# Gates as Strassen block products of normed inputs, kept in DRAM, with the state-space chunks between them

## The chip, the cores and the metric

One Trainium2 chip, one NeuronCore of it. A kernel's time is device microseconds of one execution; "before" is the median of three runs, and one further execution was profiled.

## The reference

One decoder layer on x of 1024 tokens by 1024 columns, float32. Cut to what matters here:

```python
h = rms_norm(x, norm1_g)
proj = h @ w_in                       # columns: u | q (3 groups) | k | v | conv input | g (3 x 1024)
y_s = s5_branch(u, ...)               # diagonal complex state space, gelu, @ w_ssm_glu, GLU
y_a = dilated_attention(q, k, v) @ w_att_up
y_c = conformer_conv(cv, ...)         # GLU, 31-tap causal conv, LayerNorm, silu, @ w_conv_pw2
gate = sigmoid(g + b_gate).reshape(bsz, seq, 3, 1024)
merged = gate[:, :, 0] * y_s + gate[:, :, 1] * y_a + gate[:, :, 2] * y_c
x = x + merged @ w_out
h = rms_norm(x, norm2_g)
z = h @ w_ffn_in
x = x + (silu(z[..., :2816]) * z[..., 2816:]) @ w_ffn_out
out = rms_norm(x, final_g)
```

## The kernel before

Tokens lie along the free axis (two halves of 512), features along the 128 partitions; a 1024-column operand is eight tiles of 128x1024. Every product is computed to float32 accuracy from float32r parts: each operand is split into a high part (ScalarE copy, `whi`) and the rest (subtraction on GpSimd or VectorE, `wlo`), and three matmuls, high by high, high by low and low by high, are summed in PSUM (`gemms`, L191 to L205). One block of weights is four 128x128 tiles: one load, one ScalarE copy (L104), one GpSimd subtraction (L105), and then 24 matmuls of 512 columns when both halves of the tokens are done.

The stages, in the order of the program: the input norm (`norm1`, L317), whose right sides are `hh` and `hl`, x times its gain and not yet divided by the root mean square; that factor, `rb`, is multiplied in when a product leaves PSUM. Then, for four pairs of heads, projections, attention (`attend0`, `attend1`), the 31-tap convolution on VectorE (`conv`, 31 operations of 1024 columns for each quarter) and the merge of the attention groups (`merge`, L499). Then the input of the state space (`project_u`, L609), the tables of its rotations (`s5_tables`, L778), the convolution's LayerNorm (`conv_norm`, L573, traced at high priority), and the stage of the state space (`s5_stage`, L632). This last one runs eight chunks of the state space (`s5`, L800, a generator with four parts: coefficients; transposes and kernel; states and scans; outputs) in between units of branch work, the number of units in a chunk given by `SHARE`. A unit is one 128-column block of a branch with its gate: `gate` (L920) is 48 matmuls on `hh`, `hl`, a VectorE multiplication by `rb` and a ScalarE tanh for each half, and the branch's own product is 24 matmuls. Branch c (convolution) and a (attention) are done so; branch s (state space, 48 matmuls for the two halves of its GLU) follows alone (`branch_s`, L960). There are 24 gates, eight for each branch. Then the output projection, the second norm, and the feed-forward part.

The feed-forward part already uses Strassen's scheme in Winograd's form on pairs of blocks: `left_sides` (L114) makes four sums of weight blocks for each pair (VectorE, L127) and splits seven left operands, `wino` (L152) runs seven block products of 12 matmuls into four PSUM banks, `right_sides` and `norm2` (L1015) make the sums of the token halves. Plainly done, the same pair takes 96 matmuls; so done, 84.

The order on each engine is made by a planner from the program's order as priority and an estimate of each operation's time; each engine then works its list strictly in order. `issue_after` ties instructions behind a given one on its engine. Loads and stores are issued in order by SP's queue, a few by ScalarE's. Tiles come from pools stacked from the left and from the right of the memory; a tile that takes the place of an older one waits until that one has been read for the last time.

Of the kernel before, what the change touches and what calls it, by code (L numbers as in the profile page):

```python
# [28 lines left out]
GAHEAD = 4  # L29
SHARE = (2, 2, 4, 2, 1, 2, 1, 1)  # L30
# [56 lines left out]
class Body:  # L87
    def __init__(self, tc, ins, out):
        self.tc, self.nc, self.i, self.out = tc, tc.nc, ins, out
        nc = tc.nc  # L90
        self.V, self.A, self.G, self.PE = nc.vector, nc.scalar, nc.gpsimd, nc.tensor
        self.ahead = []
        self.bufs = {"wraw": 2, "whi": 3, "wlo": 3, "t2": 4, "g": 4, "s": 2, "pt": 1, "pv": 1, "l": 16}
# [151 lines left out]
    def run(self):  # L245
        tc, nc, V, A, G, PE = self.tc, self.nc, self.V, self.A, self.G, self.PE
        with ExitStack() as st:
# [3 lines left out]
            early, banks = ExitStack(), ExitStack()  # L251
            self.wp = early.enter_context(tc.tile_pool(name="w", bufs=1, side="right", reuse_waits="tile"))
            self.pp = banks.enter_context(tc.tile_pool(name="ps", bufs=1, space=PSUM, reuse_waits="tile"))
            self.consts()
            pool = lambda name, side="left": tc.tile_pool(name=name, bufs=1, side=side, reuse_waits="tile")
            right = ExitStack()
            with pool("s5c") as self.sc, pool("h") as self.hp:
# [3 lines left out]
                with pool("at4") as self.ap4, pool("at1") as self.ap1, pool("at2") as self.ap2, pool("at3") as self.ap3, pool("at5") as self.ap5:  # L261
# [6 lines left out]
                    for hp in range(HP):  # L268
# [13 lines left out]
                self.mp = right.enter_context(pool("mg", "right"))  # L282
                with pool("gt") as self.gp, pool("br") as self.bp:
                    self.mg = [self.mp.tile([P, T], F32, tag="mg", name=f"mg{m}", bufs=KD + 1) for m in range(KD)]
# [7 lines left out]
                    self.lp = right.enter_context(pool("ml", "right"))  # L292
                    self.branch_s()
            self.lp2 = enter(pool("left"))
            self.out_proj()
            right.close()
            banks.close()
            self.bufs = {"wraw": 6, "wsum": 3, "whi": 4, "wlo": 4, "t2": 8, "ct": 6, "g": 6, "s": 2, "l": 16, "r": 20}
            self.wp = enter(pool("w2"))
            self.pp = enter(tc.tile_pool(name="ps2", bufs=1, space=PSUM, reuse_waits="tile"))  # L300
            self.early, self.enter = early, enter
            self.ffn()
            self.fill(self.rp2, 32)
# [13 lines left out]
    def norm1(self):  # L317
        nc, V, A, G, PE = self.nc, self.V, self.A, self.G, self.PE
        with self.tc.tile_pool(name="xin", bufs=1, reuse_waits="tile") as xp:
# [14 lines left out]
            self.hh = [self.hp.tile([P, T], F32R, name=f"hh{k}") for k in range(KD)]  # L334
            self.hl = [self.hp.tile([P, T], F32R, name=f"hl{k}") for k in range(KD)]
# [208 lines left out]
    def conv_in(self, ct):  # L544
        A, V = self.A, self.V
        if ct == 0:
            self.cx = {}
# [3 lines left out]
        cx = self.cx[ct] = self.ap3.tile([P, TAPS - 1 + T], F32, tag="cx", name="cx", bufs=2)  # L551
        self.G.memset(cx[:, 0:TAPS - 1], 0.0)
# [9 lines left out]
    def conv(self, ct):  # L562
        V = self.V
        cx = self.cx[ct]
# [8 lines left out]
    def conv_norm(self):  # L573
        A, V, G, PE = self.A, self.V, self.G, self.PE
        self.acts = self.act_tiles()
        for h in range(2):
            t = slice(512 * h, 512 * h + 512)
# [3 lines left out]
            ss = self.vp.tile([P, 512], F32, tag="css", name="css", bufs=2)  # L581
            V.tensor_tensor(out=ss, in0=cy[0], in1=cy[1], op=ALU.add)
            for ct in (2, 3):
                V.tensor_tensor(out=ss, in0=ss, in1=cy[ct], op=ALU.add)
            mu = self.psum("s")
            PE.matmul(mu, self.ones, ss, start=True, stop=True)
            ss = self.vp.tile([P, 512], F32, tag="css", name="css", bufs=2)
# [8 lines left out]
            bc = self.rstd([ss], BW)  # L596
# [688 lines left out]
```

## Time and profile before

| | |
|---|---|
| median of three runs | 1868.55 us (1859.29 to 1868.56) |
| the profiled execution | 1869.71 us, its span 1867.9 us |
| mean granted TensorE clock | 0.971 |
| TensorE matmuls | 8524, busy 96% of the span |
| VectorE, ScalarE, GpSimd busy | 64%, 36%, 42% |
| HBM read, written | 149.57 MB, 55.54 MB |

Spans inside the trace are counted from its first instruction. TensorE's matmuls overlap in the record: a row's duration is longer than the distance from one start to the next. A clock of 1.00 is 2.4 GHz, and 0.50 is 1.2 GHz. The stages: input norm and first projections up to about 130 us, attention to about 550, `project_u` to about 600, gates with state-space chunks to about 905, branch s to about 1080, output projection to about 1190, feed-forward to the end.

### The profile page before, as it was taken

How to read it: one execution, taken by the hardware profiler on the slowest of the kernel's cores; microseconds unless marked ns; L12 is line 12 of the kernel's file. 1: busy time of each engine (PE TensorE's matmuls, PEld its weight loads, DVE VectorE, ACT ScalarE, POOL GpSimd, SP SyncE). 2: the span in 40 equal slices, each digit the busy share in tenths (PEclk: the TensorE clock that was granted, in tenths of full speed). 3: DMA queues.
4: the chain of work that ended last, by engine and by line, in shares of the span. 5: the costliest groups of instructions: out<-in, count | busy, mean ns of one | idle time of the engine just before them, and what ended most of it. 6: DMA issues, size and time to landing. Idle time of an engine off the chain costs nothing. (4 is left out here: it accounts for less than half of the span.)

```text
span 1867.9 us, 24041 instructions
## 1 busy us (share of the span) xinstructions
PE 1798.2 (96%) x8524; PEld 1415.7 (76%) x8524; DVE 1203.5 (64%) x2010; ACT 673.1 (36%) x1280; POOL 775.7 (42%) x649
## 2 busy tenths in 40 slices
PE   7989999999999999999999999989999999999997
PEld 5867675766757778888888888757888888788876
DVE  7964767837757674764343332798888777755556
ACT  5303314223240432322332333544454555533332
POOL 5522222322222153444322234764555555467671
PEclk9989899989999899999999999989999999999998
DMA  4430110210104232322311154313444444477752
GB/s 165 131 101 30 40 57 12 68 51 11 52 18 151 69 92 78 96 81 75 95 57 51 45 186 141 130 51 119 153 158 147 163 153 164 162 269 270 266 177 90
DMA packets 118248, 206.69 MB, mean 111 GB/s; under 512 B 12264, under 2 KB 53864, under 8 KB 118128
## 3 DMA queue, kind: packets, MB, share of 16 engines
q1 hardware_dynamic: 114224, 198.86, 31.6%
q10 hardware_dynamic: 3904, 6.29, 0.9%
q8 instruction: 67, 1.10, 0.2%
q14 instruction: 53, 0.43, 0.1%
HBM read 149.57 MB, written 55.54 MB: 110 GB/s over the span
## 5 line engine op out<-in xcount | busy, mean ns | idle before, releaser
L105 POOL TENSOR_TENSOR wlo<-wraw,whi 128x512 fp32r<-128x512 f32 x185 | 256.4, 1387 | 575.8 <-ACT whi L104 565.5
L202 PE MATMUL ps<-hh,whi 128*128 128x512 f32 x832 | 338.3, 407 | 9.1 <-ACT whi L104 6.5
L204 PE MATMUL ps<-hh,wlo 128*128 128x512 f32 x832 | 334.8, 403 | 8.5 <-POOL wlo L105 8.5
L203 PE MATMUL ps<-hl,whi 128*128 128x512 f32 x832 | 337.3, 406 | 4.1 <-DVE hl L340 4.1
L104 ACT ACTIVATE whi<-wraw 128x512 fp32r<-128x512 f32 x183 | 115.4, 631 | 503.2 <-PE ps L203 391.3
L166 PE MATMUL ps<-f,whi 128*128 128x512 f32 x616 | 242.5, 394 | 5.4 <-DVE f L111 3.2
L165 PE MATMUL ps<-f,whi 128*128 128x512 f32 x616 | 242.0, 393 | 5.1 <-ACT f L110 3.3
L111 POOL TENSOR_TENSOR wlo<-wsum,whi 128x512 fp32r<-128x512 f32 (+2 forms) x144 | 187.3, 1303 | 126.4 <-ACT whi L110 66.1
L202 PEld LDWEIGHTS ps<-hh,whi 128*128 128x128 f32 x832 | 161.4, 194 | 49.1 <-issue 9.2
L204 PEld LDWEIGHTS ps<-hh,wlo 128*128 128x128 f32 x832 | 161.0, 193 | 48.2 <-POOL wlo L105 8.9
L203 PEld LDWEIGHTS ps<-hl,whi 128*128 128x128 f32 x832 | 161.2, 194 | 42.1 <-DVE hl L340 6.1
L111 POOL TENSOR_TENSOR wlo<-wraw,whi 128x512 fp32r<-128x512 f32 (+2 forms) x107 | 140.8, 1317 | 122.6 <-ACT whi L110 67.0
L569 DVE SCALAR_TENSOR_TENSOR cy<-cx,hcw,cy 128x1024 f32<-128x1024 f32 x120 | 167.8, 1398 | 0.7
L168 PE MATMUL ps<-f,wlo 128*128 128x512 f32 x616 | 166.4, 392 | 0.0
L166 PEld LDWEIGHTS ps<-f,whi 128*128 128x128 f32 x616 | 116.5, 189 | 32.9 <-DVE f L111 4.7
L165 PEld LDWEIGHTS ps<-f,whi 128*128 128x128 f32 x616 | 116.4, 189 | 32.4 <-ACT f L110 5.4
L168 PEld LDWEIGHTS ps<-f,wlo 128*128 128x128 f32 x616 | 116.8, 190 | 24.2
L110 ACT ACTIVATE whi<-wsum 128x512 fp32r<-128x512 f32 (+2 forms) x144 | 83.1, 579 | 100.5 <-PE ps L166 83.7
L165 PE MATMUL ps<-g,whi 128*128 128x512 f32 x280 | 110.0, 393 | 3.5 <-DMA g<-ad 3.1
L166 PE MATMUL ps<-g,whi 128*128 128x512 f32 x280 | 109.6, 392 | 0.0
L111 DVE TENSOR_TENSOR g<-ct,g 128x512 fp32r<-128x512 f32 x79 | 78.6, 1002 | 44.0 <-ACT g L110 43.9
L202 PE MATMUL ps<-ah,whi 128*128 128x512 f32 x256 | 99.8, 390 | 0.0
(280 smaller groups left out, 3197.9 us busy)
## 6 DMA issues: line engine op xcount, KB each, us to landing
ad<-g SPq DMA_DIRECT2D x65, 512.0 KB
g<-ad SPq DMA_DIRECT2D x65, 512.0 KB
wraw<-in_win SPq DMA_DIRECT2D x120, 256.0 KB
wraw<-in_wffi SPq DMA_DIRECT2D x96, 256.0 KB
wraw<-in_wffo SPq DMA_DIRECT2D x48, 192.0 KB
wraw<-in_wout SPq DMA_DIRECT2D x32, 256.0 KB
wraw<-in_wglu SPq DMA_DIRECT2D x16, 256.0 KB
xa<-in_xt SPq DMA_DIRECT2D x8, 512.0 KB
```

The costliest lines, as they stand in the source:

```text
L104: eng.tensor_copy(hi, raw) if eng else self.A.activation(hi, raw, AF.Copy)
L105: self.G.tensor_tensor(out=lo, in0=raw, in1=hi.bitcast(F32), op=ALU.subtract)
L110: self.A.activation(hi, src, AF.Copy)
L111: eng.tensor_tensor(out=lo, in0=src, in1=hi.bitcast(F32), op=ALU.subtract)
L165: PE.matmul(o, hi[:, k, :], xh, start=first and k == 0, stop=False, skip_group_check=not first)
L166: PE.matmul(o, hi[:, k, :], xl, start=False, stop=False, skip_group_check=not first)
L168: self.mm = PE.matmul(o, lo[:, k, :], xh, start=False, stop=k == n - 1, skip_group_check=not first).ins
L202: self.PE.matmul(o, hi[:, k, :], xh[k0 + k][:, t], start=first, stop=False)
L203: self.PE.matmul(o, hi[:, k, :], xl[k0 + k][:, t], start=False, stop=False)
L204: self.mm = self.PE.matmul(o, lo[:, k, :], xh[k0 + k][:, t], start=False, stop=last).ins
L569: V.scalar_tensor_tensor(out=cy, in0=cx[:, j:j + T], scalar=self.hcw[:, ct * TAPS + j:ct * TAPS + j + 1], in1=cy, op0=ALU.mult, op1=ALU.add)
```

## The change

The gates are computed in twelve pairs of 128-column blocks, each as seven block products on sums of the normed inputs: four row blocks of x are read from DRAM again, multiplied by gain and `rb`, summed, and split (`early_sides` for products 5, 6 and 4 during `project_u`; `late_sides` for 1, 2, 3 and 7 after it, in the place of `hh` and `hl`). Gates go through a tanh to DRAM (`gd`, stored from ScalarE's queue) and are loaded again in the branches, which now come after all gates, in the order a, s, c. The chunks of the state space run between the block products of gates, eight products to a chunk. The tables of rotations are made before the last merge; the convolution's norm is made in steps between the units of branches a and s. The weights' pool of the feed-forward part (six raw buffers, four `whi`, four `wlo`) is opened before `project_u`, so the old one of two, three and three ends there. The convolution's two padded inputs become fixed tiles, zeroed once.

```diff
+GATES = tuple((8 * b + m, 8 * b + m + 1) for b in (1, 0, 2) for m in range(0, 8, 2))
+CHUNK = 8
...
+                        else:
+                            self.s5_tables()
                         if hp % 2:
                             self.merge(hp // 2)
                         self.conv(hp)
+                early.close()
+                self.bufs.update({"wraw": 6, "wsum": 3, "whi": 4, "wlo": 4, "t2": 8, "ct": 6, "l": 16, "r": 20})
+                self.wp = enter(pool("w2", "right"))
+                self.tp = right.enter_context(pool("t", "right"))
+                with pool("xn") as self.xp, pool("uw") as self.up:
                     self.project_u()
-                    with pool("tb") as self.sp:
-                        self.s5_tables()
-                    with pool("cn") as self.vp:
-                        with tc.high_priority():
-                            self.conv_norm()
-                    with pool("s5") as self.sp:
-                        self.s5_stage()
-                    self.branch_s()
+                    begun = self.first_products()
+                    for p in (1, 2, 3):
+                        self.late_sides(p)
+                with pool("s5") as self.sp:
+                    self.gate_stage(begun)
+                self.bp = right.enter_context(pool("br", "right"))
+                self.acts_a()
+                self.last_gates()
+            self.mp = left.enter_context(pool("mg"))
+            with pool("cn") as self.vp:
+                self.branches()
+            self.lp = left.enter_context(pool("ml"))
+            self.last_branch()
...
+    def block(self, k, h):
+        b = self.xp.tile([P, 512], F32, tag="xb", name="xb", bufs=8)
+        self.nc.sync.dma_start(out=b, in_=self.i["xt"][k][:, HALVES[h]])
+        return b, k, h
+    def normed(self, block):
+        b, k, h = block
+        self.V.scalar_tensor_tensor(out=b, in0=b, scalar=self.vec(C_N1 + k), in1=self.rb[:, HALVES[h]], op0=ALU.mult, op1=ALU.mult)
+        return b
+    def early_sides(self, blocks):
+        V = self.V
+        b11, b12, b21, b22 = (self.normed(b) for b in blocks)
+        V.tensor_tensor(out=b11, in0=b12, in1=b11, op=ALU.subtract)
+        self.side(5, b11, self.G)
+        V.tensor_tensor(out=b22, in0=b22, in1=b11, op=ALU.subtract)
+        self.side(6, b22, V)
+        V.tensor_tensor(out=b21, in0=b21, in1=b22, op=ALU.subtract)
+        self.side(4, b21, self.G)
+    def late_sides(self, p):
+        V, G = self.V, self.G
+        if p < 3:
+            for k, b in enumerate([self.block(k + KB * (p - 1), 0) for k in range(KB)]):
+                self.side(p, self.normed(b), V if k % 2 else G)
+            return
+        for k in range(KB):
+            b22 = self.normed(self.block(k + KB, 1))
+            b12 = self.normed(self.block(k, 1))
+            self.side(3, b22, V)
+            V.tensor_tensor(out=b12, in0=b22, in1=b12, op=ALU.subtract)
+            self.h7 = getattr(self, "h7", []) + [b12]
+        for b12 in self.h7:
+            self.side(7, b12, G)
...
+        def add(key, b, u, h):
+            def f(banks):
+                x, m = r[key], GATES[n][u]
+                V.tensor_tensor(out=x, in0=banks[b], in1=x, op=ALU.add)
+                A.activation(x, x, AF.Tanh, scale=0.5, bias=self.hbg[:, m:m + 1])
+                self.nc.scalar.dma_start(out=self.gd[m, :, HALVES[h]], in_=x)
+            return f
...
+        after = {1: copy("m", "u"), 5: copy("y", "y"), 2: add("m", "v", 0, 0), 6: copy("n", "u"), 4: copy("z", "z"), 3: add("n", "y", 0, 1), 7: end}
+        ticked = {p: (lambda banks, f=f: (f(banks), self.tick())) for p, f in after.items()}
+        return self.wino(make, KB, self.h1, ticked, banks, only), r
+    def first_products(self):
+        make = self.gate_left(0)
+        begun = [(make, *self.gate_pair(0, make, only=(5, 4)), (1, 2, 6, 3, 7))]
+        for n in (1, 2):
+            begun.append((None, *self.gate_pair(n, self.gate_left(n), only=(4,)), (1, 5, 2, 6, 3, 7)))
+        for p in (1, 2, 6):
+            make(p, keep=True)
+        return begun
...
+        put(4, 0)
+        put(7, 0)
+        for e in range(n):
+            t = 7 + CHUNK * e
+            put(t + 3, e + 1)
+            put(t + CHUNK, e)
+            put(t + CHUNK, e + 1)
+            put(t + CHUNK, e + 2)
...
+    def gate(self, m, b):
+        t = self.tp.tile([P, 2, 512], F32, tag="t1", name="gate", bufs=4).rearrange("p a b -> p (a b)")
+        self.nc.sync.dma_start(out=t, in_=self.gd[8 * b + m])
         return t
```

`gate_left` hands `left_sides` the four weight blocks of a pair; `gate_stage` advances the parts of the chunks by the numbers that `put` notes, one tick after each block product, each with `issue_after` the last matmul; `acts_a` and `acts_s` split the branches' inputs; `branches` and `last_branch` are the old units without their gate's matmuls.

## Rows read from the trace of the kernel before

**Rows 1.** The page, busy time of each engine over the span.
```profile
PE 1798.2 (96%) x8524; PEld 1415.7 (76%) x8524; DVE 1203.5 (64%) x2010; ACT 673.1 (36%) x1280; POOL 775.7 (42%) x649
```
**Rows 2.** Windows: length, busy PE, PEld, DVE, ACT, POOL, clock, DMA share, GB/s.
```profile
704.10:901.90 197.80, 197.80 (x1045) 163.80 (x1044) 118.68 (x237) 55.44 (x96) 82.89 (x78) 1.00 0.29 81
1330.00:1600.00 270.00, 270.00 (x1193) 223.65 (x1192) 208.14 (x254) 135.71 (x235) 142.52 (x100) 1.00 0.44 156
```
**Rows 3.** Timeline of TensorE, start and duration, two neighbours in a gate's product.
```profile
659.65 0.39 PE L202 MATMUL ps<-hh,whi 128*128 128x512 f32 x1
659.88 0.39 PE L203 MATMUL ps<-hl,whi 128*128 128x512 f32 x1
```
**Rows 4.** Waits of TensorE from 560 to 700: total us, times, longest.
```profile
PE ps L586 <- DVE css L584: 5.3, 1, 5.3
PE ps L853 <- POOL gm L809: 2.8, 1, 2.8
PE ps L217 <- DVE css L595: 1.6, 1, 1.6
...
```
**Rows 5.** TensorE from 600 to 680: the window, two of three lines, one slow matmul.
```profile
600.00:680.00 80.00, 68.73 (x290) 0.87 0.31 97
L203 PE MATMUL ps<-hl,whi 128*128 128x512 f32 x76 | 32.7, 430 | 0.0
...
L204 PE MATMUL ps<-hh,wlo 128*128 128x512 f32 x75 | 31.1, 415 | 0.0
673.40 0.80 PE L204 MATMUL ps<-hh,wlo 128*128 128x512 f32 x1
```
**Rows 6.** Lines of TensorE from 1200 to 1250, where `norm2` makes sums.
```profile
L166 PE MATMUL ps<-f,whi 128*128 128x512 f32 x51 | 22.6, 443 | 5.4 <-DVE f L111 3.2 <-POOL f L111 2.2
L165 PE MATMUL ps<-f,whi 128*128 128x512 f32 x50 | 21.3, 430 | 3.3 <-ACT f L110 3.3
L168 PE MATMUL ps<-f,wlo 128*128 128x512 f32 x48 | 14.6, 430 | 0.0
```
**Rows 7.** Sums by VectorE in that stretch, beside GpSimd and not.
```profile
L1043 DVE TENSOR_TENSOR ct<-xa 128x512 f32<-128x512 f32 x4 | 5.8, 1468 | 0.0
L1046 DVE TENSOR_TENSOR xa<-xa,ct 128x512 f32<-128x512 f32 x4 | 2.6, 679 | 0.0
```
**Rows 8.** VectorE: a `uw` copy; windows of table lines L794 and L796; convolution's L569.
```profile
585.85 1.12 DVE L623 TENSOR_TENSOR uw<-ps,rb 128x512 f32<-128x512 f32 x1
545.00:600.00 55.00, 9.16 (x28) 0.94 0.35 114
...
545.00:600.00 55.00, 12.72 (x28) 0.94 0.35 114
491.00:545.00 54.00, 1.30 (x1) 1.00 0.07 24
```
**Rows 9.** The block products' helpers from 1330 to 1600, by line.
```profile
L111 POOL TENSOR_TENSOR wlo<-wsum,whi 128x512 fp32r<-128x512 f32 x58 | 80.9, 1397 | 59.7 <-ACT whi L110 30.8 <-PE ps L168 26.6 <-PE ps L166 2.2
L127 DVE TENSOR_TENSOR wsum<-wraw 128x512 f32<-128x512 f32 x29 | 26.2, 903 | 1.3 <-POOL wlo L111 1.3
L1094 DVE TENSOR_TENSOR m<-ps,m 128x512 f32<-128x512 f32 x15 | 10.2, 682 | 2.0 <-PE ps L168 2.0
```
**Rows 10.** The chunks' lines: TensorE 704.1 to 901.9; VectorE (first, last), GpSimd 660 to 960.
```profile
L202 PE MATMUL ps<-hh,whi 128*128 128x512 f32 x144 | 57.1, 397 | 0.0
L204 PE MATMUL ps<-ah,wlo 128*128 128x512 f32 x105 | 40.9, 390 | 0.0
L905 DVE TENSOR_TENSOR es<-x,zw 64x254 f32<-64x254 f32 x32 | 18.7, 585 | 0.7
...
L895 DVE MEMSET es<- 128x4 f32 x8 | 0.5, 62 | 5.6 <-PE ps L912 5.6
L807 POOL TENSOR_TENSOR gm<-bb,pw 128x256 f32<-128x256 f32 x16 | 15.0, 955 | 0.2 <-PE ps L853 0.2
```
**Rows 11.** The load of `cn` and VectorE's wait for it.
```profile
605.30 0.69 DVE L582 TENSOR_TENSOR css<-cn 128x512 f32<-128x512 f32 x1 [6.58 <-DMA cn<-cd]
```

More of the change, by code (lines that the diff above doesn't have):

```diff
@@ new lines, in run @@
+                with pool("s5") as self.sp:
[8 more added lines that the diff above has]
+            self.last_branch()
+            right.close()
+            self.lp2 = enter(pool("left", "right"))
@@ L546, in conv_in @@
         if ct == 0:
-            self.cx = {}
+            self.cx = [self.ap3.tile([P, TAPS - 1 + T], F32, name=f"cx{c}") for c in range(2)]
+            for cx in self.cx:
+                self.G.memset(cx[:, 0:TAPS - 1], 0.0)
             self.cd = [self.dp.tile([P, T], F32, name=f"cd{c}") for c in range(KB)]
@@ L580, in conv_norm @@
                 self.nc.sync.dma_start(out=cy[ct], in_=self.cd[ct][:, t])
[L581 removed]
+            cn.append((cy, self.vp.tile([P, 512], F32, tag="css", name="css", bufs=2)))
+        yield
+        for cy, ss in cn:
             V.tensor_tensor(out=ss, in0=cy[0], in1=cy[1], op=ALU.add)
@@ L584, in conv_norm @@
                 V.tensor_tensor(out=ss, in0=ss, in1=cy[ct], op=ALU.add)
+        yield
+        for cy, ss in cn:
             mu = self.psum("s")
-            PE.matmul(mu, self.ones, ss, start=True, stop=True)
-            ss = self.vp.tile([P, 512], F32, tag="css", name="css", bufs=2)
+            with self.tc.issue_after(self.mm):
+                PE.matmul(mu, self.ones, ss, start=True, stop=True)
             for ct in range(KB):
@@ new lines, in blocks, with side @@
+    def blocks(self, k):
+        return [self.block(kk, h) for kk in (k, k + KB) for h in range(2)]
+    def normed(self, block):
+        b, k, h = block
+        self.V.scalar_tensor_tensor(out=b, in0=b, scalar=self.vec(C_N1 + k), in1=self.rb[:, HALVES[h]], op0=ALU.mult, op1=ALU.mult)
+        return b
+    def side(self, p, src, eng):
+        pool, tag, n = {5: (self.tp, "t0", 8), 6: (self.tp, "t0", 8), 4: (self.tp, "t1", 4)}.get(p, (self.hp, "h", 2 * KD))
+        z = pool.tile([P, 2, 512], F32R, tag=tag, name=f"e{p}", bufs=n)
+        self.split(src, z[:, 0], z[:, 1], eng)
+        self.h1.setdefault(p, []).append((z[:, 0], z[:, 1]))
@@ new lines, in branches, with gate @@
+    def branches(self):
+        V, A, G = self.V, self.A, self.G
+        self.mg = [self.mp.tile([P, T], F32, tag="mg", name=f"mg{m}", bufs=KD + 1) for m in range(KD)]
+        order = [(m, b) for b in (1, 0, 2) for m in range(KD)]
+        gts = {u: self.gate(*u) for u in order[:2]}
+        def gate(m, b):
+            n = order.index((m, b)) + 2
+            if n < len(order):
+                gts[order[n]] = self.gate(*order[n])
+            return gts.pop((m, b))
+        self.next_gate = gate
+        norm = self.conv_norm()
+        next(norm)
+        for m in range(KD):
+            gt = gate(m, 1)
+            for t, ps in zip(HALVES, self.gemm(self.i["watt"][m], *self.act_a)):
+                V.scalar_tensor_tensor(out=self.mg[m][:, t], in0=gt[:, t], scalar=1.0, in1=ps, op0=ALU.add, op1=ALU.mult)
+            if m == 2:
+                act = self.acts_s()
+            if m % 2:
+                next(norm)
+        for m in range(KD):
+            gt = gate(m, 0)
+            pa = self.gemm(self.i["wglu"][m], *act)
+            pb = self.gemm(self.i["wglu"][8 + m], *act)
+            for h, t in enumerate(HALVES):
+                f = self.tmp([P, 512])
+                A.activation(f, pb[h], AF.Tanh)
+                V.scalar_tensor_tensor(out=f, in0=f, scalar=1.0, in1=pa[h], op0=ALU.add, op1=ALU.mult)
+                V.scalar_tensor_tensor(out=f, in0=gt[:, t], scalar=1.0, in1=f, op0=ALU.add, op1=ALU.mult)
+                G.tensor_tensor(out=self.mg[m][:, t], in0=self.mg[m][:, t], in1=f, op=ALU.add)
+            next(norm, None)
```

201 lines of the change are left out of this document (92 added, 109 removed).

## The prediction

> **What bounds the kernel now.** I read the page's busy times first: TensorE is busy for 96% of the span, and the next, VectorE, for 64% [rows 1]. The reader is to see an engine that hardly ever waits, so what counts is its number of matmuls, and the few places where it stands still. What a matmul costs is not its row's 390 ns: neighbours start 0.23 us apart and overlap [rows 3], and a stretch without waits holds 1193 of them in 270.0 us [rows 2], 0.2263 us each. Then I read TensorE's waits and the windows around `project_u` and the first gates: three of its five waits there are on the convolution's norm and two on the first chunk's coefficients, 11.2 us together [rows 4]. From 600 to 680 the clock averages 0.87 [rows 5]. From 704 to 902, where gates, branch units and chunks run together, TensorE is busy for the whole window at clock 1.00, and VectorE for 118.7 of 197.8 us [rows 2].
>
> **Gates.** 24 gates of 48 matmuls are 1152. Twelve pairs of 7 products of 12 are 1008. 144 fewer at 0.2263 us: -32.6 us. This lies on the bounding engine, and nothing takes its place there: the sums are made by VectorE, the splits by ScalarE and GpSimd.
>
> **The old stall.** From 600 to 680 there are 226 matmuls of 512 columns [rows 5], 51.1 us at full rate; the norm's and the first chunk's small matmuls take some 8 us. About 21 us of 80 are lost: 11 to the waits, 10 to matmuls at 1.2 GHz after them (one of 0.80 us in [rows 5], a long way over 0.39). The change puts the norm in steps between branch units, each behind the last matmul issued, where VectorE has little to do, and the tables ahead of the last merge. I count -21 us, and what is late next by itself, as follows.
>
> **The start of the block products.** This is the term that I can't read off. Thirty-two quarter blocks of x are loaded, and VectorE makes 32 normed tiles, 16 sums, and 12 of the 28 low parts: 60 operations, with eight `uw` copies of 1.12 us [rows 8] among them. Alone such an operation takes 0.68 us, beside GpSimd up to 1.47 [rows 7]. So they need 9 + 60 x 0.68 = 50 us, or 97 us. Add about 11 us for the first pair's sums and the first chunk's coefficients. By the sizes of the pools, the x tiles take the place of the attention's results, which are free after the last merge, near 565. `project_u` ends on TensorE near 600; the four products started first and the five that are left of the first pair end at 600 + 9 x 12 x 0.2263 = 624. So VectorE has some 57 us for 61 to 108. Products of the second pair can fill in only until the four PSUM banks are taken, 5.4 us. Loads add to it: a tile of 256 KB was waited for some 4 us after its issue, and VectorE stood 6.58 us [rows 11]. From below this costs nothing: with uncontended operations the lag is about one product, and the pairs begun cover it. From above, at a mean of 1.0 us, 80 us of work in 57 leave 18 us after the fill, and the clock falls behind such waits: 28 us. The nearest row is the same preparation ahead of the feed-forward part. From 1200 to 1250 stand 149 matmuls [rows 6], 33.7 us of work in 50: 16.3 us lost, of which 8.7 are waits. I take +15.
>
> **Tables and convolution.** The tables, some 31 us of VectorE from 545 to 600 in three lines of 28 operations [rows 8], now rank above the last quarter's convolution, which today is done but for one operation by 491 [rows 8]. The two will share VectorE with the last attention, whose softmax steps wait behind an operation of at most 1.3 us. And that attention loses fillers: weights for `project_u` come from the new pool, part of which lies where v and k were. Between 0 and 8 us; I take +3, since that stretch holds few fillers today.
>
> **The steady stage.** A chunk is now eight products, 96 matmuls, 21.7 us, and its own matmuls. In seven chunks [rows 2], three lines of 144 and three of 104 or 105 [rows 10] make 745 matmuls, 168.6 us; the other 29 us are 4.2 for each chunk. So 25.9 us a chunk, where it is 28.3 now. VectorE: the chunks' 16 lines come to 116.6 us, 14.6 for each [rows 10]; eight sevenths of a pair bring 4.6 sums at 0.90 and 4.6 additions from PSUM at 0.68 [rows 9], 7.3 us. Together 21.9 of 25.9: VectorE stays under TensorE. GpSimd has eight splits of 1.4 us [rows 9], 11.2, and some 5 us for a chunk's coefficients (five lines, 42 us for eight chunks, the first in [rows 10]): 16 of 25.9. Ends: 0 and +18 (below, third rival); I take +2. The gates' stores and loads through DRAM (25 MB), and the blocks of x read again (8 MB), pass beside it. The stores go by ScalarE's queue, where the tanh is waited for on the same engine, and a branch unit needs only one load of 512 KB in 5.4 us or more. I cost these at nothing; their cover is TensorE's queue of work, and if it were gone, one load's delay of some 4 us at the start of the branches would show. The norm's steps there: +1. Weights, with six raw buffers, no longer wait for each other: nothing, since TensorE does not wait for them from 704 on.
>
> **The sum**, against the profiled execution's 1869.7 (span 1867.9 and 1.8 around it): -32.6 - 21 + 15 + 3 + 2 + 1 = -32.6 (the last five cancel by chance), so 1837.1. That execution is 1.2 us above the median of the runs, so I say 1836.
>
> **A rule weighed.** The gate sums take 0.90 us on average [rows 9] where the same operation alone takes 0.68, and sums in the feed-forward start take 1.47 [rows 7]. The Trainium skill (SBUF — State Buffer, "Who interferes with whom") says that a VectorE instruction with two SBUF inputs and a GpSimd instruction that reads SBUF lock each other out, the later one waiting for the whole of the other. By that rule, the trace agrees: 1.47 is 0.68 and most of a GpSimd operation. It speaks against the change, which moves weight preparation onto just such operations. What that would make of the time is worked out from rows in the third rival.
>
> **The rivals.** First, a clean start: the planner has the sides ready in time and the first chunk waits for nothing. Then +15 becomes nothing: 1821. For it: `project_u` leaves VectorE and ScalarE idle today once the tables are out. Against it: 61 us in 57 at the very best.
>
> Second, slower: TensorE waits at the entries of the chunks. Each chunk's transposes, state products and outputs stand in TensorE's queue behind a fixed product; what they read comes from VectorE and GpSimd, which are now busier, and all later products wait behind them. The first chunk did this today: 3.4 us of waits and slow matmuls after, some 6 us [rows 4, 5]. There are 24 entries. From a mean of 1.8 us on each (42 us in all) the kernel is slower than 1878; at 2.5 us it is 1836 + 60 = 1896. Against it: the seven later chunks waited for nothing [rows 2].
>
> Third, VectorE becomes the bound of the start and of the stage, because operations on two tiles stretch beside GpSimd, as [rows 7] show. Chunk operations stretched by a fifth (17.5 us), sums at 1.47 (6.8) and additions at 0.68 (3.1) make 27.4 us a chunk against 25.9, and at a third more stretch 29 to 30: 12 to 31 us over eight chunks, say 18. With 28 for the start: 1869.7 - 32.6 - 21 + 28 + 3 + 18 + 1 - 1.2 = 1865.
>
> **How the numbers follow.** Forecast, 1824 to 1852: 0.64. Clean start: 0.15. VectorE bound, 1852 to 1875: 0.14. Waits at the entries, over 1878: 0.07. A measurement can tell about 0.5%, 9.3 us, from no change. Faster than 1859.2 are the first two and a little under half of the third: 0.85; within, the rest of the third: 0.08; slower: 0.07. The range 1816 to 1862 leaves out the slower rival, the upper part of the third, and little below: two terms can't save more than 32.6 and 21.
>
> **What would show it.** 144 fewer matmuls of 512 columns, and block products in place of gates, with 96 matmuls and 26 us to a chunk. No wait on `css` or `sm` in the branches of over 1 us. Waits of TensorE on the tiles e1, e2, e3 and e7, with a clock under 1, within 50 us of `project_u`'s end, adding to some 15 us lost; nothing like it later. It is wrong if TensorE's loss from the last attention to the first three pairs is over 30 us or under 8, if the stage's windows show TensorE idle at each chunk, or if VectorE is busy for over nine tenths of it.

## The result, and the profile after

The changed kernel takes 1879.8 us (median of 20 runs, 1871.8 to 1882.2) where the kernel before takes 1867.6 on the same chip: a ratio of 1.0064, 95% interval 1.0048 to 1.0080. It is slower by 12 us, 0.6%; 1836 was forecast, and the range ended at 1862. The profiled span is 1875.5 us against 1867.9.

The page's busy times, the line that answers to [rows 1]:

```profile
PE 1777.2 (95%) x8380; PEld 1392.3 (74%) x8380; DVE 1303.8 (70%) x2110; ACT 728.7 (39%) x1390; POOL 865.9 (46%) x707
```

The 144 matmuls are gone (8524 to 8380). What came back is read best by counting: take the time at which n matmuls of 512 columns have been issued on TensorE's timeline (the start of the one that follows the n-th), and subtract n times 0.2263 us, the rate of [rows 2]. What is left is time not spent at that rate, small matmuls included. Both kernels issue 1536 such matmuls up to the end of `project_u`; 84 block products of 12 end at the 2544th, the branches at the 3312th (before: at the 3456th), the four matmuls of 512 columns in the convolution's norm not counted.

```
us above the rate            before   after   forecast of the difference
up to the 1536th              249.8   266.8     +3
1536th to end of branches      61.8    88.2     -3   (-21 +15 +2 +1)
output projection to the end   68.1    64.9      0
144 matmuls fewer                             -32.6
```

So 14 us of the miss lie before the end of `project_u`, and 29 behind it. In the changed kernel the 88.2 divide into 32.1 for the first twelve products (1536th to 1680th), 49.1 for the 72 that follow, and 7.0 in the branches. TensorE's waits from 490 to 800 us (us in total, times, longest), as [rows 4] showed those of before:

```profile
PE ps L166 <- ACT n L710: 10.0, 4, 5.0
PE ps L166 <- DVE uw L644: 6.5, 1, 6.5
PE ps L459 <- DVE stat L430: 5.8, 1, 5.8
PE ps L166 <- ACT z L710: 3.9, 1, 3.9
PE ps L166 <- ACT m L710: 3.2, 2, 2.5
PE ps L972 <- POOL gm L927: 2.3, 1, 2.3
```

The windows of the start (length, then busy time and count of PE, PEld, DVE, ACT, POOL; clock; DMA share; GB/s), and the stretch that [rows 2] showed for before:

```profile
600.00:620.00 20.00, 18.96 (x84) 15.27 (x82) 19.97 (x22) 5.47 (x9) 11.04 (x7) 1.00 0.51 161
620.00:640.00 20.00, 9.41 (x30) 6.75 (x31) 20.00 (x21) 8.76 (x16) 12.59 (x9) 0.80 0.55 167
640.00:660.00 20.00, 14.34 (x49) 10.76 (x49) 19.07 (x18) 7.46 (x15) 16.82 (x14) 0.84 0.46 160
704.00:902.00 198.00, 191.10 (x1010) 157.18 (x1010) 151.65 (x253) 92.18 (x165) 106.83 (x95) 0.99 0.42 128
```

Two things are to be seen. VectorE is busy for all of 620 to 640 while TensorE has half its work and a clock of 0.80. And in the steady stretch, where before TensorE never stood, it is now idle for 6.9 of 198 us with VectorE busy for 152 of them: three quarters, not a bound. Four of TensorE's waits, the largest sum, are on a ScalarE copy out of PSUM (`n`, L710), which takes 0.6 us. What ScalarE itself waited for, from 690 to 925:

```profile
ACT m L717 <- DVE m L716: 41.3, 9, 8.0
ACT n L717 <- DVE n L716: 39.1, 10, 7.7
ACT z L717 <- DVE z L716: 8.5, 5, 4.9
```

L717 is the tanh of a gate, L716 the sum on VectorE that it needs. ScalarE stood 89 us at such tanh. One of them in the order of its list:

```profile
750.64 0.63 ACT L111 ACTIVATE whi<-wsum 128x512 fp32r<-128x512 f32 x1
759.31 0.72 ACT L717 ACTIVATE m<-m,hbg 128x512 f32<-128x512 f32 x1 [8.04 <-DVE m L716]
760.06 0.33 ACTq L718 DMA_DIRECT2D gd<-m  x1
760.51 0.63 ACT L111 ACTIVATE whi<-wraw 128x512 fp32r<-128x512 f32 x1 [0.48 <-ACT m L717]
761.05 0.58 ACT L710 ACTIVATE n<-ps 128x512 f32<-128x512 f32 x1
```

The sum stood on VectorE behind a chunk's coefficients (it began at 758.59). Behind the tanh stand the split of the next weights and the copy that frees a PSUM bank; TensorE had used up both and waited 5.05 us at 761.68, and its clock fell to 0.91 from 760 to 780.

### The profile page after: what moved, and what is told of

The parts are those of the page before. It is cut to its first block, busy times and chain, and to the rows that moved or that the text cites. A ratio compares the mean times of both kernels' runs of the same rounds, so it can differ in the third digit from the quotient of the medians.

```text
span 1875.5 us, 24385 instructions
## 1 busy us (share of the span) xinstructions
PE 1777.2 (95%) x8380; PEld 1392.3 (74%) x8380; DVE 1303.8 (70%) x2110; ACT 728.7 (39%) x1390; POOL 865.9 (46%) x707
## 5 line engine op out<-in xcount | busy, mean ns | idle before, releaser
L106 POOL TENSOR_TENSOR wlo<-wraw,whi 128x512 fp32r<-128x512 f32 x137 | 197.6, 1446 | 320.8 <-ACT whi L105 312.4
L112 POOL TENSOR_TENSOR wlo<-wsum,whi 128x512 fp32r<-128x512 f32 (+2 forms) x192 | 251.4, 1313 | 196.9 <-ACT whi L111 124.8
L112 POOL TENSOR_TENSOR wlo<-wraw,whi 128x512 fp32r<-128x512 f32 (+2 forms) x143 | 190.1, 1330 | 173.3 <-ACT whi L111 106.4
L105 ACT ACTIVATE whi<-wraw 128x512 fp32r<-128x512 f32 x135 | 84.6, 630 | 338.3 <-PE ps L204 225.7
L203 PE MATMUL ps<-hh,whi 128*128 128x512 f32 x448 | 186.6, 417 | 17.6 <-DVE kn L417 7.8
L204 PE MATMUL ps<-hl,whi 128*128 128x512 f32 x448 | 186.3, 417 | 4.1 <-DVE hl L349 4.1
L205 PE MATMUL ps<-hh,wlo 128*128 128x512 f32 x448 | 184.0, 411 | 0.0
L166 PE MATMUL ps<-e,whi 128*128 128x512 f32 x336 | 138.8, 413 | 25.4 <-ACT n L710 10.0
L167 PE MATMUL ps<-e,whi 128*128 128x512 f32 x336 | 135.7, 404 | 1.2 <-POOL e L112 1.2
L203 PEld LDWEIGHTS ps<-hh,whi 128*128 128x128 f32 x448 | 88.9, 198 | 42.8 <-issue 15.9
L111 ACT ACTIVATE whi<-wraw 128x512 fp32r<-128x512 f32 (+2 forms) x143 | 84.6, 592 | 87.0 <-PE ps L167 58.7
```

Source lines behind the costliest of these rows:

```text
L105: eng.tensor_copy(hi, raw) if eng else self.A.activation(hi, raw, AF.Copy)
L106: self.G.tensor_tensor(out=lo, in0=raw, in1=hi.bitcast(F32), op=ALU.subtract)
L111: self.A.activation(hi, src, AF.Copy)
L112: eng.tensor_tensor(out=lo, in0=src, in1=hi.bitcast(F32), op=ALU.subtract)
L166: PE.matmul(o, hi[:, k, :], xh, start=first and k == 0, stop=False, skip_group_check=not first)
L167: PE.matmul(o, hi[:, k, :], xl, start=False, stop=False, skip_group_check=not first)
```

## The experiments

All ratios are to the kernel before, 95% intervals. The medians come from several chips, so kernels are compared by their ratios. The columns behind them are us above the rate, counted as above, in the one profiled run of each.

```
                         median  ratio [interval]         to 1536  -1680  -2544  -3312
after                    1879.8  1.0064 [1.0048, 1.0080]   266.8    32.1   49.1    7.0
e1_no_tables             1872.0  1.0026 [0.9995, 1.0058]   257.3    32.1   49.1    7.1
e2_old_pool              1890.3  1.0111 [1.0064, 1.0158]   273.4    20.8   49.7    9.5
e3_no_normed             1868.8  0.9992 [0.9962, 1.0022]   270.0    21.6   48.3    7.7
e4_chunk9                1884.5  1.0090 [1.0060, 1.0120]   269.1    32.1   52.7    9.1
e5_tables_later          1880.1  1.0075 [1.0042, 1.0108]   260.8    29.6   61.5    7.7
e6_tanh_later            1860.2  0.9956 [0.9924, 0.9988]   262.9    32.2   32.2    5.8
e7_raw_sides             1865.6  0.9988 [0.9957, 1.0020]   262.9    25.6   33.4   21.9
e8_raw_pools             1861.7  0.9983 [0.9952, 1.0013]   263.9    19.7   32.3   19.8
e9_raw_all               1885.7  1.0108 [1.0069, 1.0148]   281.1     3.9   37.4   25.8
e10_tables_gpsimd        1889.8  1.0135 [1.0102, 1.0167]   302.1    32.2   32.2    5.8
e11_early_weights        1909.6  1.0228 [1.0198, 1.0258]   291.6    33.5   38.6   10.6
e12_raw_tables_early     1860.2  0.9990 [0.9963, 1.0017]   278.2     2.6   32.2   21.7
e13_early_all_normed     1873.0  1.0068 [1.0042, 1.0095]   280.3    32.1   32.2    5.8
e14_no_fill              1899.7  1.0198 [1.0169, 1.0227]   273.4    31.0   52.3    7.5
e15_tables_early         1873.5  1.0061 [1.0033, 1.0089]   281.9    32.1   32.2    5.8
e16_raw_tables_behind    1845.2  0.9893 [0.9860, 0.9926]   257.1     5.3   32.2   27.9
e17_raw_tables_before    1849.1  0.9889 [0.9851, 0.9928]   261.6     6.9   32.2   27.2
e18_tables_behind        1860.6  0.9963 [0.9941, 0.9986]   261.3    31.7   33.5    5.9
```

The first column scatters by some 6 us between kernels whose edits all lie behind it (after, e4, e6); the others hardly at all.

**The steady stage: e6, e4.** e6 moves only the tanh into the branches, and with it the stores from ScalarE's queue to SP's:

```diff
-                A.activation(x, x, AF.Tanh, scale=0.5, bias=self.hbg[:, m:m + 1])
-                self.nc.scalar.dma_start(out=self.gd[m, :, HALVES[h]], in_=x)
+                self.nc.sync.dma_start(out=self.gd[m, :, HALVES[h]], in_=x)
...
+    def finish(self, m, b, t):              # in the branches, one unit ahead
+        self.A.activation(t, t, AF.Tanh, scale=0.5, bias=self.hbg[:, 8 * b + m:8 * b + m + 1])
```

> The changed kernel, only the 48 tanh of the gates moved: the sums go to DRAM (stores from SP's queue), and ScalarE makes the tanh on whole 128x1024 tiles in the branches. Theory for the steady stage: ScalarE stands at a tanh until VectorE's sum is done, with the next split of weights behind it; without that the 49 us above the matmuls' rate from the 1680th to the 2544th matmul fall to 38 to 44, and the kernel takes 1869 to 1875 us. Rival, the sums on VectorE or the copies out of PSUM are late by themselves: 48 to 50 us there, 1878 to 1882.

From 49.1 us to 32.2, more than the theory said, and 1860 us: this alone makes the change faster than the kernel before. The same 20 us windows, first after, then e6:

```profile
720.00:740.00 20.00, 18.53 (x100) 15.07 (x99) 14.00 (x22) 7.94 (x14) 13.66 (x13) 1.00 0.44 134
740.00:760.00 20.00, 16.63 (x80) 13.19 (x79) 19.66 (x36) 8.71 (x16) 10.15 (x11) 1.00 0.41 120
```

```profile
720.00:740.00 20.00, 20.00 (x115) 16.53 (x114) 19.73 (x32) 7.86 (x15) 11.36 (x12) 1.00 0.48 156
740.00:760.00 20.00, 20.00 (x115) 16.54 (x113) 19.54 (x35) 8.53 (x16) 10.63 (x9) 1.00 0.46 138
```

VectorE is busier in e6, nearly full, and TensorE does not wait at all. And ScalarE's waits there are now on TensorE, which is to give a weight buffer back:

```profile
ACT whi L111 <- PE ps L167: 81.2, 51, 2.5
```

So the stage was not short of VectorE; its order tied ScalarE, and through it the weights, to VectorE's list. Tanh and stores were moved together; which of the two holds ScalarE was not tried apart, but the waits of after stand at the tanh.

e4 (`CHUNK = 9`) gives the stage more room for each chunk:

> The changed kernel with a chunk of the state-space part every 9 block products instead of 8. Theory 1 for the stage: VectorE's and ScalarE's work per product falls by a ninth of the chunk's share, the waits on the PSUM copies (3.8 at 689 and 5.1 at 762) get smaller, and of the 12 us lost there 4 to 8 are saved: 1872 to 1876 us. Rival, each chunk's entry costs its wait whatever the distance, or the loss is only what the start left behind: 1878 to 1881.

Both expectations failed by the time, and the 4 to 8 us were not saved. Of the 52.7 us in the column, 4.5 pass between the last block product and the first matmul of the branches, which waits for an operand that ScalarE splits behind the last two tanh and their stores:

```profile
PE ps L203 <- ACT ah L1054: 4.8, 2, 4.3
```

The block products themselves lose 48.2 us, against 49.1. Room does not help where order is what binds.

**The start: e3, e7, e8, e12, e16.** e3 leaves out the 32 normed products:

```diff
     def normed(self, block):
         b, k, h = block
-        self.V.scalar_tensor_tensor(out=b, in0=b, scalar=self.vec(C_N1 + k), in1=self.rb[:, HALVES[h]], op0=ALU.mult, op1=ALU.mult)
         return b
```

> The changed kernel without the 32 VectorE operations that multiply the quarter blocks of x by gain and norm (the blocks are loaded and summed as they are; the gates are no longer right). Theory 1: 32 operations at a mean of some 0.85 us are 27 us out of a list that is full from 580 to 660, and the 35 us lost at the start fall to 10 to 18: 1855 to 1863 us. Rival, the loads of x are late (they begin at 577 and DMA moves some 160 GB/s there): the sides come at the same time, 1875 to 1880.

10.5 of 32 us came back, neither expectation. The trace tells why: a copy out of PSUM for which TensorE waited 3.9 us in the changed kernel and 3.6 us in e3 stands on ScalarE behind splits of sides, there for VectorE's normed tiles, here for the loads. First after, then e3:

```profile
636.79 0.63 ACT L111 ACTIVATE e<-xb 128x512 fp32r<-128x512 f32 x1 [3.47 <-DVE xb L662]
639.17 0.58 ACT L710 ACTIVATE z<-ps 128x512 f32<-128x512 f32 x1
```

```profile
634.25 0.63 ACT L111 ACTIVATE e<-xb 128x512 fp32r<-128x512 f32 x1 [4.99 <-DMA xb<-in_xt]
634.79 0.58 ACT L709 ACTIVATE z<-ps 128x512 f32<-128x512 f32 x1
```

So in the start, too, ScalarE's order ties TensorE to what its splits wait for. e7 takes more of the work away, and has e6's edit in it:

```diff
+        A.activation(b11, b11, AF.Copy, scale=g)          # x times its gain, without rb
+        A.activation(b12, b12, AF.Copy, scale=g)
+        V.tensor_tensor(out=b11, in0=b12, in1=b11, op=ALU.subtract)                              # side 5
+        V.scalar_tensor_tensor(out=b12, in0=b22, scalar=g2, in1=b12, op0=ALU.mult, op1=ALU.subtract)   # 7
+        V.scalar_tensor_tensor(out=b22, in0=b22, scalar=g2, in1=b11, op0=ALU.mult, op1=ALU.subtract)   # 6
+        V.scalar_tensor_tensor(out=b21, in0=b21, scalar=g2, in1=b22, op0=ALU.mult, op1=ALU.subtract)   # 4
+        self.h1[p] = [(self.hh[k0 + k][:, t], self.hl[k0 + k][:, t]) for k in range(KB)]         # p = 1, 2, 3
...
+    def finish(self, m, b, t):
+        self.V.tensor_tensor(out=t, in0=t, in1=self.rb, op=ALU.mult)                              # then the tanh
```

> Three edits at once, nothing left out. The block products run on x times its gain, not yet divided by the root mean square: sides 1, 2 and 3 are then the tiles that the projections already use, sides 5, 6, 4 and 7 take 16 loads, 16 VectorE operations and 16 splits (32 normed products, 16 sums and 28 splits before), and the factor is multiplied in, with the tanh, on whole tiles in the branches. Products 1 and 2 of two pairs start first and need nothing new. The tables are made behind project_u. Theory 1, VectorE's list bounded the start: the 32 us lost from the 1536th to the 1680th matmul fall to 8 to 14, 1680 is reached at 645 to 655 us, and the kernel takes 1840 to 1855 us. Rival, loads, the chunk's own coefficients or the weights' splits bound the start: 20 us or more are still lost there and the time stays above 1860.

> The kernel with sides of raw x, and the attention's pools stacked in another order, so that the tiles for x lie where masks, keys and weights of the softmax were and not where the attention's results wait for their stores: loads of x can begin near 550 instead of 577. If loads that come late still cost anything at the start: 3 to 8 us less than the kernel with sides of raw x alone. If VectorE or the chunk sets it: within 2 us of that kernel.

By its time e7 came out as the rival had it, with 25.6 us lost at the start. e8's edit is the order of the pools (`at1, at2, at4, at3, at5`): 5.9 us less at the start, as if loads that came late did cost something there; by the ratios it is 1 us, well inside the intervals, so the time does not show it. But in both the tables, traced behind `project_u`, now filled VectorE in the place of the normed products, and the multiplication by `rb` cost the branches 14 to 16 us, which no expectation had. e12 and e16 move the tables out of the start:

```diff
-                        else:
-                            self.s5_tables()
                         if hp % 2:
                             self.merge(hp // 2)
                         self.conv(hp)
+                        if hp in (1, 2):          # e12, e13, e15: half of the tables each
+                            self.s5_tables(hp)
+                    self.s5_tables()              # e16, e18, in its place
```

> Sides of raw x, the other order of pools, the weight pool cut in two at the old alignment (the 32 bytes of filling stay in the pool of the split weights), the norm's factor on GpSimd in branch a, and the tables made by VectorE in four parts behind the convolutions of the second and third attention. Theory 1: the 1536th matmul is reached at 590 to 600 us, from there to the 1680th 4 to 8 us are lost (3.9 in the kernel with the tables on GpSimd), matmuls stand 0.2267 us apart again: 1818 to 1832 us. Rival, the late place of the sides or the chunk costs the start 15 us again: 1835 to 1845.

> Sides of raw x, the other order of pools, the weight pool cut in two, the tables traced behind the last convolution (so that the planner fits them into VectorE's gaps in the last attention and merge, some 26 and 20 us by the windows of the kernel without tables), and gates in the branches finished two units ahead instead of one. Theory 1: the 1536th matmul at 598 to 606 us, 3 to 5 us lost from there to the 1680th, 8 to 14 in the branches: 1822 to 1836 us. Rival, the tables cost 10 us or more wherever VectorE makes them, late ones hold up the sides: 1840 to 1850.

> The same with the tables ahead of the last merge, as the change put them: the 1536th matmul at 606 to 612 us, the rest as in the other: 1830 to 1842 us. If the place makes no difference, within 3 us of the other.

All three times are above what theory 1 had, for the branches' sake and, in e12, for the tables' place; e16's lies in its rival's range, but its loss is in the branches and not at the sides. The start is about as theory 1 had it: the first twelve products lose 2.6, 5.3 and 6.9 us, of which some 2.7 are the first chunk's own matmuls (28 of the 44 small ones in a chunk, which take 4.3 us in e6). e16 and e17 differ only in the tables' place, and their ratios are alike. The windows of e16, to be held against 600 to 660 above:

```profile
600.00:620.00 20.00, 19.93 (x89) 16.20 (x88) 18.44 (x18) 7.16 (x14) 17.51 (x16) 1.00 0.38 112
620.00:640.00 20.00, 17.84 (x96) 13.97 (x95) 16.39 (x23) 9.82 (x21) 15.63 (x16) 1.00 0.38 122
640.00:660.00 20.00, 20.00 (x96) 16.26 (x96) 19.71 (x32) 7.64 (x13) 15.72 (x15) 1.00 0.41 134
```

e16 and e17, at 0.989 of the kernel before, beat both kernels, by 20 us and more. They still lose 27 us in the branches, where the factor is multiplied in on VectorE and GpSimd; that gates are finished two units ahead there, not one as in e12 (21.7), did not help. In e16 TensorE waits there (of its waits from 470 to 1090 us, those at the branches' lines) for

```profile
PE ps L204 <- DVE t L1119: 4.2, 6, 2.1
PE ps L204 <- ACT gate L1042: 3.1, 1, 3.1
PE ps L204 <- ACT t L1103: 3.1, 4, 1.6
PE ps L204 <- DVE mg L1092: 2.7, 3, 1.8
```

**The tables: e1, e5, e10, e15, e18.** e1 leaves their 84 operations out:

> The changed kernel with the 84 VectorE products and sums of the two tables left out (their tiles are filled by one GpSimd memset each, stores and loads stay; the state-space output is no longer right). Theory 1, VectorE's list is overfull from the last attention on: the last attention goes from 52 us back to 44 to 48, merge and project_u lose a few us less, and the kernel takes 1866 to 1873 us against 1880. Theory 2, what is late there is the weights, whose new pool comes free only as the attention's tiles do: the last attention may gain up to 3 us, merge and project_u stay at 65 us, 1877 to 1880. If the start of the block products is bound by VectorE at a fixed end near 660, what is gained before it is partly waited off there: then 1874 to 1878.

9.5 us less by the 1536th matmul, 7 by the ratios; as theory 1 had it. TensorE's wait on `stat` falls from 5.8 us to 1.1. The other four make them elsewhere (e5 behind `project_u`; e10, e15 and e18 on top of e6, on GpSimd or at the places in the diff above):

> The changed kernel with the two tables made behind project_u in the program's order (nothing left out) instead of ahead of the last merge. Theory 1, VectorE has no free time from 470 to 665: the last attention gets back its 8 us as without the tables, but the start of the block products pays them again; TensorE is at its 1680th matmul of 512 columns at 675 to 685 us (679 in the changed kernel, 670 without the tables), the whole 1876 to 1884. Rival, only the place inside the attention's chain of small steps was costly: 1868 to 1873, as without the tables.

> The changed kernel with the tanh in the branches, and the tables made by GpSimd instead of VectorE, at the same place ahead of the last merge. Theory 1, the tables cost by VectorE's time: as without the tables, 8 to 10 us less than with the tanh moved alone: 1848 to 1854 us. Rival, GpSimd's operations on two tiles hold up VectorE's convolution and the attention's additions in turn: 1857 to 1862.

> The changed kernel with the tanh in the branches and the tables in the second and third attention (same VectorE work, 168 operations of half the size). Theory 1: VectorE has idle time there (165 us busy of 240), so that the result is that of leaving the tables out, 8 to 10 us less than with the tanh moved alone: 1849 to 1854 us. Rival, the tables delay the convolution and the softmax there as they did in the last attention: 1857 to 1865.

> The changed kernel with the tanh in the branches, and the tables traced behind the last convolution. Theory 1: the last attention gets its 8 us back, but the normed sides need VectorE up to 660 and the tables' rest stands among them: 1852 to 1860 us. If VectorE's gaps before 580 hold them all: 1847 to 1852.

e5: the time is theory 1's, the place is not; 8.5 us are saved up to the 1680th and 12.4 more lost behind it. Part of both is that the first chunk's entry, behind the 1632nd matmul in the changed kernel, comes behind the 1722nd in e5, since VectorE is at the tables until 681 us; the chunk's own matmuls and TensorE's waits for `gm` (5.8 us) go with it. e18: nothing gained on e6. e15 is slower than either expectation: 19 us more than e6 are lost by the 1536th, about half of them between 368 and 415 us, the rest where 19 operations of the last convolution stand from 470 us on (10 in e6); what each of the waits came from was not taken apart, but idle time summed over 240 us was no free time. e10, too, misses both: it costs 39 us between the two profiled runs, 33 by the ratios, and the reason is the one of the steady stage, on another engine. TensorE's longest wait from 470 to 620, and then the tables' groups of instructions on GpSimd there (count, busy us, mean ns, idle before):

```profile
PE ps L205 <- POOL wlo L106: 25.4, 2, 16.2
```

```profile
L914 POOL TENSOR_TENSOR tab<-tab,tabw 128x32 f32<-128x32 f32 (+6 forms) x25 | 16.2, 647 | 1.1
L913 POOL TENSOR_TENSOR tabw<-tab,cs 128x32 f32<-128x32 f32 (+6 forms) x24 | 15.1, 631 | 1.3
L912 POOL TENSOR_TENSOR tab<-tab,cs 128x64 f32<-128x64 f32 (+6 forms) x22 | 13.6, 627 | 0.1
```

The low parts of `project_u`'s weights stood behind 45 us of tables.

**Late weights: e2, e11, e13.** e2 keeps the attention's weight pool for `project_u`; e11 and e13 cut the new pool in two, raw, high and low weights in the place of the old pool (e11 on top of e10, e13 of e15):

> The changed kernel with the attention's weight pool kept: project_u takes its weights from it as before, and the new pool holds only what is added to it (the same 50 KB in all, the buffers taken in turn from both). Theory 2, late weights are the loss: merge and project_u go from 65 us back to 52 to 55, units of project_u fill the last attention again, and the kernel takes 1867 to 1871 us. Theory 1, VectorE sets the end of the start: project_u ends on TensorE up to 10 us earlier, but the block products still wait for their sides, so that the first three pairs are through at the same time; 1876 to 1880.

> The kernel with the tanh in the branches and the tables on GpSimd, and the new weight pool cut in two, so that project_u's weights need not wait for the last attention's values. Theory 2, late weights cost the merge and project_u some 7 us: 6 to 9 us less than without this edit, 1840 to 1847. Theory 1, VectorE, with 32 normed products, sets the end of the start: project_u ends up to 10 us earlier, the first block products wait that much longer, and the time is within 3 us of that kernel.

> Normed sides as in the changed kernel; tanh in the branches, tables in the second and third attention, weight pool cut in two at the old alignment. Theory 1, with 32 normed products on VectorE the start's end is fixed: TensorE is at the 1680th matmul within 4 us of the same kernel with one pool, whatever project_u gains, and the two differ by less than 4 us: 1845 to 1853. Theory 2, late weights are a loss of their own: 6 to 9 us less than that kernel.

In e2 `project_u` began early enough to fill gaps of the attention (the matmul behind the 1344th, its first, at 493 instead of 552 us), and nothing of it stayed: TensorE then stood from 600 to 610 altogether, at a weight split on ScalarE, which stood at a side whose block VectorE had not made. The window, and the waits from 490 to 630:

```profile
600.00:610.00 10.00, 0.00 (x0) 0.00 (x0) 9.90 (x12) 3.40 (x6) 4.85 (x4) 0.50 0.61 176
```

```profile
PE ps L212 <- ACT whi L114: 15.6, 1, 15.6
ACT e L120 <- DVE xb L687: 16.2, 4, 6.2
```

e13 and e15 differ by 1.6 us, within the scatter: in this setting late weights are not a loss of their own. e13 does not test a fixed end of the start, since `project_u` did not end earlier; but e10 and e18 end it 40 us apart, and 32 us follow in both, so that the start's loss moves with `project_u`: its work is too long, not its end fixed. The times of e2, e9 and e11 are not to be read for weights, for the reason that follows (e2 had it in part, 0.2305 us from one matmul to the next). But e11's count can be read: 10.5 us less than e10 by the 1536th, more than that column's scatter, and 33.5 behind it, 1 of them by the rate. Where the tables are on GpSimd, the earlier weights did gain what theory 2 said, in the one profiled run of each:

> The kernel with sides of raw x and the other order of pools, with three more edits: the tables are made by GpSimd in the last attention, the new weight pool is cut in two so that the buffers of raw, high and low weights lie where the old pool lay and not where the last attention's values are, and GpSimd multiplies the gates of branch a by the norm's factor. Theory 1: the 1536th matmul of 512 columns, at 611 us in that kernel, is reached at 595 to 600, the 20 us lost from there to the 1680th fall to 6 to 12, the 20 us lost in the branches to 10 to 14: 1828 to 1842 us. Rival, the first chunk's own coefficients and transposes cost the start its 20 us whatever VectorE has to do beside them: 1845 to 1855.

e9 has its tables on GpSimd (45 us at `project_u`) and its matmuls at 0.2333 us from there on; its time is outside both expectations. Only its start answers a question: 3.9 us, so the first chunk's coefficients do not cost 20 whatever VectorE has to do.

**The address: e14.**

```diff
             self.ffn()
-            self.fill(self.wp, 32)
```

> The changed kernel without the 32 bytes that fill up its weight pool, so that the weights and the tiles below them lie 32 bytes higher; no instruction changes. If the address is what slowed the matmuls: 0.233 to 0.234 us from one to the next from project_u on, some 30 us in all, 1905 to 1915. If it was the order of the pools or the buffers' number: 1878 to 1882.

There are two runs of e14. Its ratio is 1.3% over the changed kernel's, 25 us; the address it is, with less than the 30 us and the 0.233 us that were expected. The same window of the feed-forward part, after and e14:

```profile
1400.00:1500.00 100.00, 100.00 (x443) 82.81 (x442) 76.58 (x93) 51.35 (x88) 50.76 (x37) 1.00 0.43 153
```

```profile
1400.00:1500.00 100.00, 100.00 (x433) 80.92 (x432) 71.18 (x90) 50.34 (x85) 49.43 (x36) 1.00 0.43 152
```

Ten matmuls fewer in 100 us, with no wait and a clock of 1.00 in both.

## Why the prediction was wrong

**The gates, -32.6: right.** 144 matmuls fewer, and 0.2267 us from one to the next.

**The old stall, -21: right, as far as it shows.** No wait on `css` or `sm` is left ahead of the products or in the branches, which lose 7.0 us. No run measures the 21 alone; the sum below closes with it.

**The start, +15: the mechanism right, the size wrong.** 32.1 us are lost, of which some 2.7 are the chunk's own, so 29: a little over the upper end of the term (28), not its middle. The forecast took less than 1.0 us for each of VectorE's 60 operations, and read 1.47, a mean of four, as the most that one can take. From 580 to 660 they took 1.03:

```profile
L662 DVE SCALAR_TENSOR_TENSOR xb<-xb,vecs,rb 128x512 f32<-128x512 f32 x32 | 34.5, 1113 | 0.7 <-DMA xb<-in_xt 0.7
L112 DVE TENSOR_TENSOR e<-xb,e 128x512 fp32r<-128x512 f32 x12 | 12.5, 1047 | 0.0
```

(with the 16 sums, L675 to L693, at 15.0 us). They lay between 0.68 and 1.79 us each; the longest, at 587.44 us, has a GpSimd split beside it from 586.99 to 588.67. The Trainium skill (SBUF — State Buffer, "Who interferes with whom") has the later of two such operations wait for the whole of the other, and the trace agrees; that no run here takes GpSimd alone out leaves the rule itself untested. e12 and e16 bear the term out: the loss is gone there. But they took away more than these operations: sides 1 to 3 are ready beforehand, other products come first, pools and tables are moved. e3, with 32 of the 60 operations left out and nothing else, brings back 10.5 us, and its loads then hold up ScalarE; how much of the 29 is VectorE's alone was not told apart.

**Tables and convolution, +3: wrong in size.** 17 us were lost up to the 1536th matmul. 9.5 are the tables (e1; 7 by the ratios): TensorE waits 5.8 us on `stat` up to 503 and has a clock of 0.69 from 500 to 520. The forecast let the softmax wait "behind an operation of at most 1.3 us"; but it is behind as many of them as rank above it. Some 7.5 us stay open, about as much as that column scatters; whether late weights are in it is not shown (1.6 us between e15 and e13, 10.5 between e10 and e11).

**The steady stage, +2: the step that failed.** The sum of VectorE's work was right in kind (21.9 us of 25.9; 152 of 198 were measured), and so its conclusion, VectorE under TensorE. The error is the sentence on the stores: "the tanh is waited for on the same engine", costed at nothing under "TensorE's queue of work". That queue is fed by splits that stand behind this very tanh on ScalarE. 16.9 us, shown by e6. That this lies within the term's ends, 0 and +18, is luck: the upper end was for VectorE as the bound. No rival had it: the second put the waits at the chunks' entries, which cost 4.3 us at the first chunk and nothing later, and that the time lies in its range, over 1878, is luck too; the third, at 1865, had the start nearly right (28) and named VectorE for the stage, where e6 has it fuller and TensorE without a wait.

**The rest, 0:** 3.2 us less from the output projection on, not forecast and not looked into.

Together: 14 before `project_u`'s end, 14 in the start and 15 in the stage, less 3 at the end: 40 us, from the 1835.3 us of span that the sum amounts to, to 1875.5. Of the signs that the forecast named for being wrong, the first came: 17 us up to `project_u`'s end and 29 in the first twelve products are over 30. TensorE did not stand at each chunk, and VectorE was busy for 77% of the stage.

## What to carry to other kernels

An engine's share of busy time says nothing of what stands behind a wait in its list. Before putting an operation that waits for another engine onto the engine that also prepares the bound engine's operands, name the preparation that stands behind it, and give the waiting operation to a stage where nothing urgent follows. Work moved into an engine's idle time is free only if what ranks behind it there is not waited for: the tables cost in four places (after, e5, e10, e15), and whether they do behind the last convolution (e16, e18) is within the scatter. For operations on two tiles beside GpSimd, take the mean of the nearest busy stretch (1.0 us here), not that of the operation alone.

## What the runs showed of the hardware

Where the operands lie changed the matmuls' rate: shifted by 32 bytes, a matmul of 512 columns came 0.2320 us after the last, not 0.2267, and with the pool cut in two and the 32 bytes of filling in its other part 0.2333 (e9, e11), at a clock of 1.00 and without waits. That is 2 to 3% of every matmul from there on: 25 us in e14, where the change was to bring 32. Whether the split weights, or the sides that lie below them in memory, are what has to be placed so was not told apart.
